# Two-layer mixer and chunk attention: where x's split parts are kept, when projection weights are listed, and how the output steps are spread

## The chip, the cores and the metric

The kernel runs on one core of one Trainium2 chip. The metric is the time of one execution in device microseconds (us). A profiled execution gives, beside its time, a span: from its first to its last instruction on the core.

## The reference

`x` is 2048 rows of 1024 float32. Cut to what matters here:

```python
# layer A
h = rms_norm(x, a_norm_g);  u, v, z = split(h @ w_in, 3)       # 3 x 2048 columns
v = layer_norm(gelu(v));    mixed = per-head 128x128 mixing of v, + b_s
x = x + (gelu(u) * mixed * silu(z)) @ w_out
# shared keys and values, from the same x
k, v = split(rms_norm(x, g_kv) @ w_kv, 2)                        # 16 heads of 64
# layer B: each chunk of 64 rows attends to itself and the 8 chunks before it
h = rms_norm(x, b_norm_g);  q, z = split(h @ w_qz, 2)
p = softmax(q * scale @ k.T + relative bias);  o = p @ v
x = x + (o * silu(z)) @ w_out
return rms_norm(x, final_norm_g)
```

## The kernel before

**Products.** Every float32 product is made of three matmuls of rounded parts (`mm3`, L112): an operand is split into a high part (ScalarE copies it into float32r) and a low part (VectorE subtracts the high part), and high x high, high x low and low x high are summed in one PSUM bank. The large products (layer A, values, layer B's output) use Strassen's scheme: seven sub-products, called phases, `PHS = (1, 7, 2, 6, 5, 4, 3)`, each with two 128-row parts `jp` here.

**Stages.** Layer A comes first and the change leaves it alone. Then the rows go through in four tiles `t` of 512 rows, each of four blocks `b` of 128 rows.

*Value stage.* For each tile, `norm` loads a block of x and normalizes it, `block` transposes it on TensorE and copies the transposed block back in place (`xf[t, b]`, 128 x 8 x 128), and `strassen("vp")` multiplies it with the value weights: 14 products of 4 steps, one step being one `mm3`. Before each product `v_left` splits its left operand with `split_s` into two tiles of the tag `S`, of which the pool `vp` has 8. The operand is a 128 x 512 half of a block as it is (phases 1, 2, 4), or a sum that GpSimd has made in place by then (7, 6, 5, 3). `block` also stores the unsplit transposed block in DRAM (`xtd`), for the attention stage.

*Attention stage.* For each tile, `reload(t)` brings all 512 rows back as the right operands of the projections, in two tiles with one buffer each, `hh` (high parts) and `hl` (low parts): it loads a block into one of four `raw` buffers, copies on ScalarE (L168) and subtracts on VectorE (L169). For each of 8 head pairs `p`, `project` makes q and k, `gate` makes z; each such projection (`one`, 8 steps of 3 matmuls) needs one weight tile, which `weights` loads, scales by the gain where `t` is 0, and splits into two tiles of the tag `T`, 8 in all. `score` makes one 128-row block of scores and its softmax, `flip` transposes and splits it, `value` multiplies with the values.

*Output.* The product with layer B's output weights for tile t-1 (`outs[t-1]`, 56 steps) is run between the heads of tile t. Each phase takes four `T` tiles, loaded by `o_right`; its left operands are sums on four `raw` buffers (`o_left`).

**Order.** One Python loop lists the instructions: for each head pair eight rounds `u`, each with a score, a share of the steps of the generator `ahead(t, p)`, a flip, and again a share. `ahead` lists the projections of the next head pair, then `SHARE[t][p]` steps of the output; at the last head pair of a tile it lists `reload(t + 1)` first, then the output steps, then the first projections of tile t+1. A scheduler places the listed instructions on the engines' queues, so an engine's order can differ from the list; each queue then runs in order. `paced_by_pj` adds an order edge without a wait, so that a weight copy does not come ahead of a given projection matmul. All DMAs are issued from the SP queue.

Of the kernel before, what the change touches and what calls it, by code (L numbers as in the profile page):

```python
# [9 lines left out]
F32 = mybir.dt.float32  # L10
# [7 lines left out]
P = 128  # L18
S = 2048
D = 1024  # L20
KD = D // P
T = 512
NT = S // T
TB = T // P
W2 = 2048
NH = W2 // P
NPAIR = 8
# [6 lines left out]
def trunk_kernel(  # L34
# [19 lines left out]
    nc = tc.nc  # L54

    dram = ctx.enter_context(tc.tile_pool(name="dram", bufs=1, space=DRAM))
# [16 lines left out]
        for t in range(NT - 1)  # L73
    ]
    vhd = [dram.tile([P, NPAIR, TB, 256], F32, name=f"vhd{t}") for t in range(NT)]
    xtd = [[dram.tile([P, D], F32, name=f"xtd{t}_{b}") for b in range(TB)] for t in range(NT)]
    ogd = [dram.tile([P, 2, NPAIR, 2, P], F32, name=f"ogd{t}") for t in range(NT)]
    x2d = [[dram.tile([P, D], F32, name=f"x2d{t}_{b}") for b in range(TB)] for t in range(NT - 1)]

# [7 lines left out]
    kg = cst.tile([P, KD, 1], F32, name="kg")  # L87
    bg = cst.tile([P, KD, 1], F32, name="bg")
# [7 lines left out]
    sh = ctx.enter_context(tc.tile_pool(name="sh", bufs=1))  # L96
# [26 lines left out]
    sub, add = ALU.subtract, ALU.add  # L123
    tv, tg = nc.vector.tensor_tensor, nc.gpsimd.tensor_tensor
# [16 lines left out]
    def x_tiles(t):  # L141
        th = sh.tile([P, KD, T], F32R, tag="hh", name=f"hh_b{t}")
        tl = sh.tile([P, KD, T], F32R, tag="hl", name=f"hl_b{t}")
        xT[t] = [(th[:, k, :], tl[:, k, :]) for k in range(KD)]
        return th, tl

    def block(t, b):
        xt = xf[t, b]
        half = [
            banks[0].tile([P, 4, P], F32, tag="t4", name=f"tr_b{t}_{b}_{h}", bufs=4)  # L150
            for h in range(2)
        ]
        for k in range(KD):
            tpose(half[k // 4][:, k % 4, :], xt[:, k * P : (k + 1) * P], ident[:])
        x3 = xt[:].rearrange("p (k c) -> p k c", k=KD)
        for h in range(2):
            ks = slice(h * 4, h * 4 + 4)
            nc.scalar.copy(x3[:, ks, :], half[h][:])
        nc.sync.dma_start(xtd[t][b][:], xt[:])

    def reload(t):
        th, tl = x_tiles(t)
        for b in range(TB):
            xt = sh.tile([P, D], F32, tag="raw", name=f"xr_b{t}_{b}", bufs=4)
            nc.sync.dma_start(xt[:], xtd[t][b][:])
            x3 = xt[:].rearrange("p (k c) -> p k c", k=KD)
            oh = th[:, :, b * P : (b + 1) * P]
            nc.scalar.copy(oh, x3)  # L168
            tv(tl[:, :, b * P : (b + 1) * P], x3, oh.bitcast(F32), op=sub)  # L169

    pace = []
    beat = []
# [7 lines left out]
            )  # L180
        return ins

    def paced_by_pj(ins, back=2):
        if pace:
            tc.add_manual_dep(
                ins.ins, pace[-min(back, len(pace))],
                mybir.DependencyInfo(mybir.DependencyClass.NoSync, mybir.DependencyReason.DATA),
                reason="order",
            )

    def scaled(raw, gain):
# [11 lines left out]
    def raw_w(t, name):  # L203
        if t:
            return raws[0].tile([P, 1024], F32, tag="wr", name=name, bufs=2)
        return sh.tile([P, 1024], F32, tag="raw", name=name, bufs=4)

    def split_in(raw, wh, wl):
        hi = nc.scalar.copy(wh[:], raw[:])  # L209
        tv(wl[:], raw[:], wh[:].bitcast(F32), op=sub)  # L210
        return hi

    def weights(t, p, c):
        name = f"b{t}_{p}_{c}"
        raw = raw_w(t, f"raw_{name}")
        w = w_tile(f"wh_{name}"), w_tile(f"wl_{name}")
        if t:
            nc.sync.dma_start(raw[:], wk3[p][c][:])
        else:
            nc.sync.dma_start(raw[:], w_kqz[p, :, c, :])  # L220
            paced_by_pj(scaled(raw, (bg if c else kg)[:, :, :]), 3)
            nc.sync.dma_start(wk3[p][c][:], raw[:])
        hi = split_in(raw, *w)
        if t:
            paced_by_pj(hi)
        return w
# [61 lines left out]
            evict(ph, jp, ps[:])  # L288
            yield

    def split_s(pool, bufs, name, src):
        hi, lo = (
            pool.tile([P, 4, P], F32R, tag="S", name=f"S{i}{name}", bufs=bufs) for i in "hl"
        )
        nc.scalar.copy(hi[:], src)
        tv(lo[:], src, hi[:].bitcast(F32), op=sub)
        return [(hi[:, k, :], lo[:, k, :]) for k in range(4)]

    def o_sums(u, place, s_place):
# [43 lines left out]
    with ExitStack() as actx:  # L343
# [21 lines left out]
        sub, add, mul = ALU.subtract, ALU.add, ALU.mult  # L365
# [544 lines left out]
        for n in range(2, 6):  # L910
            b = start[n, 1]
# [46 lines left out]
        tv, tg = nc.vector.tensor_tensor, nc.gpsimd.tensor_tensor  # L958
# [159 lines left out]
    with ExitStack() as vctx:  # L1118
        vp = vctx.enter_context(tc.tile_pool(name="vp", bufs=1, reuse_waits="tile"))
# [16 lines left out]
        def v_left(t):  # L1136
            def raw(jp, r, h):
                return xf[t, 2 * jp + r][:, h * 512 : h * 512 + 512]

            def left(ph, jp):  # L1140
                a11, a12, a21, a22 = (raw(jp, r, h) for r in range(2) for h in range(2))
                src = {1: a11, 7: a11, 2: a12, 6: a11, 5: a21, 4: a22, 3: a12}[ph]
                out = split_s(vp, 8, f"v{t}_{ph}_{jp}", src.rearrange("p (k c) -> p k c", k=4))
                if ph == 1:
                    tg(a11, a11, a21, op=sub)
# [72 lines left out]
    with ExitStack() as bctx:  # L1218
# [16 lines left out]
        def half_tile(tag, name, bufs, dtype=F32):  # L1235
            return sb.tile([P, 512], dtype, tag=tag, name=name, bufs=bufs)

        def c_tile(name):
            return half_tile("C", name, 4)

        def one(t, p, c):
# [350 lines left out]
        def o_all(t):  # L1592
# [158 lines left out]
```

## Time and profile before

| | us |
|---|---|
| median of 3 runs | 2696.48 (2694.29 to 2697.41) |
| profiled execution | 2698.01 |
| its span | 2696.2 |
| TensorE busy in it | 2627.2 (97%) |
| value stage, tiles 0 to 3 | 1351 to 1531 |
| attention stage, tile 0 | 1531 to about 1729 |
| attention stage, tile 1 | to about 2031 |
| attention stage, tile 2 | to about 2318 |
| attention stage, tile 3, and the last output | to 2696 |

Matmuls are pipelined: one of 128 x 512 has a duration of 0.39 us in the rows while the next starts 0.23 us after it, so a matmul that is "busy" is not one that runs alone. Lost time shows as a gap in brackets at the end of a timeline row (the idle time before the instruction, and what ended it), and as matmuls that start 0.43 us apart, when the granted clock is halved (PEclk).

### The profile page before, as it was taken

To read this page: it belongs to the slowest core of one execution; us is meant where nothing else is said; L and a number is where in the kernel's file an instruction comes from. 1 tells how busy PE (TensorE), PEld (TensorE's weight loads), DVE (VectorE), ACT (ScalarE), POOL (GpSimd) and SP (SyncE) were. 2 spreads that over 40 slices of the span, in tenths; PEclk is the share of its full clock that TensorE was granted. 3 is DMA by queue.
4 is the path that set the end of the run, shared out by engine and by line. 5 is a ranking of instruction groups with operands and counts; after the bars stand their busy time and mean duration, and the time that the engine had idled before them with its cause. 6 is when DMAs were issued, how large, how long until landed. Compare 5 with 4: busy or idle time off the path is not lost.

```text
span 2696.2 us, 38071 instructions
## 1 busy us (share of the span) xinstructions
PE 2627.2 (97%) x12960; PEld 2197.9 (82%) x12960; DVE 1892.0 (70%) x2937; ACT 1296.6 (48%) x2296; POOL 888.2 (33%) x874
## 2 busy tenths in 40 slices
PE   9999999999999999999989999999999999999997
PEld 7888888888888888888878788787887888788885
DVE  5655676766777568657677767788677667766676
ACT  5422242443434435333365466676556555655553
POOL 3511335152262414015043344343332223323243
PEclk9999999999999999999999999999999999999999
DMA  7898999989888879858666687788889667766576
GB/s 293 314 326 332 342 364 326 328 306 350 331 320 281 308 259 334 301 200 273 256 238 209 216 266 232 223 294 290 281 265 295 200 220 246 242 204 193 180 236 238
DMA packets 274770, 735.53 MB, mean 273 GB/s; under 512 B 29584, under 2 KB 61328, under 8 KB 274576
## 3 DMA queue, kind: packets, MB, share of 16 engines
q1 hardware_dynamic: 274576, 733.09, 79.2%
q8 instruction: 104, 1.70, 0.2%
q14 instruction: 90, 0.74, 0.1%
HBM read 540.56 MB, written 181.93 MB: 268 GB/s over the span
## 4 chain that ended last, share of the span: by engine, by line
PE 81%; DVE 7%; DMA 6%; issue 2%; ACT 2%; POOL 2%; SPq 1%; DVEq 0%; POOLq 0%; ACTq 0%
PE P L115 11%; PE P L114 11%; PE P L113 11%; PE pj L115 5%; PE pj L113 5%; PE pj L114 5%; PE pv L1391 4%; PE Po L113 4%; PE Po L114 4%; PE Po L115 4%; PE s L1331 4%; PE tp L1366 3%; PE vp L115 1%; PE vp L113 1%; PE vp L114 1%
## 5 line engine op out<-in xcount | busy, mean ns | idle before, releaser
L113 PE MATMUL P<-T,S 128*128 128x512 f32 x1248 | 497.0, 398 | 2.1 <-ACT S L393 2.1
L115 PE MATMUL P<-T,S 128*128 128x512 f32 x1248 | 491.1, 394 | 0.0
L114 PE MATMUL P<-T,S 128*128 128x512 f32 x1248 | 490.1, 393 | 0.6 <-DVE T L396 0.6
L1350 POOL TENSOR_SCALAR pr<-pr,sl 128x640 f32<-128x640 f32 (+4 forms) x256 | 199.3, 779 | 522.9 <-DVE sl L1349 473.8
L113 PE MATMUL pj<-hh_b,wh_b 128*128 128x512 f32 x768 | 320.6, 417 | 1.6 <-ACT hh_b L168 0.8
L115 PE MATMUL pj<-hh_b,wl_b 128*128 128x512 f32 x768 | 305.9, 398 | 0.8 <-DVE wl_b L210 0.7
L114 PE MATMUL pj<-hl_b,wh_b 128*128 128x512 f32 x768 | 304.4, 396 | 0.0
L1346 ACT ACTIVATE pr<-pr,nm 128x640 f32<-128x640 f32 (+4 forms) x256 | 195.4, 763 | 193.2 <-DVE nm L1339 182.4
L115 PEld LDWEIGHTS P<-T,S 128*128 128x128 f32 x1248 | 235.8, 189 | 50.4
L113 PEld LDWEIGHTS P<-T,S 128*128 128x128 f32 x1248 | 236.2, 189 | 46.9 <-ACT S L393 2.3
L114 PEld LDWEIGHTS P<-T,S 128*128 128x128 f32 x1248 | 236.0, 189 | 46.1 <-DVE T L396 1.0
L1371 DVE TENSOR_TENSOR pt<-tp,pt 128x640 fp32r<-128x640 f32 (+4 forms) x256 | 188.7, 737 | 49.2 <-ACT pt L1370 46.2
L1339 DVE CUSTOM_DVE_ANT_0 pr<-s,bias 128x640 f32<-128x640 f32 (+4 forms) x256 | 188.0, 735 | 43.6 <-PE s L1331 36.7
L1370 ACT CAST pt<-tp 128x640 fp32r<-128x640 f32 (+4 forms) x256 | 159.1, 622 | 50.9 <-PE tp L1366 47.3
L1366 PE MATMUL tp<-ident,pr 128*128 128x128 f32 x1120 | 167.8, 276 | 10.4 <-DVE pt L1371 7.9
L115 PEld LDWEIGHTS pj<-hh_b,wl_b 128*128 128x128 f32 x768 | 145.5, 189 | 34.1 <-DVE wl_b L210 2.8
L1366 PEld LDWEIGHTS tp<-ident,pr 128*128 128x128 f32 x1120 | 131.4, 141 | 44.6 <-issue 17.0
L113 PEld LDWEIGHTS pj<-hh_b,wh_b 128*128 128x128 f32 x768 | 146.5, 191 | 20.1 <-ACT wh_b L209 1.6
L1391 PEld LDWEIGHTS pv<-pt,V 128*128 128x128 f32 x896 | 144.2, 190 | 20.2 <-ACT pt L1370 2.6
L114 PEld LDWEIGHTS pj<-hl_b,wh_b 128*128 128x128 f32 x768 | 146.6, 191 | 17.1
L1391 PE MATMUL pv<-pt,V 128*128 128x256 f32 (+3 forms) x896 | 154.4, 321 | 2.7 <-ACT pt L1370 1.8
L210 DVE TENSOR_TENSOR wl_b<-raw_b,wh_b 128x1024 fp32r<-128x1024 f32 x96 | 125.8, 1311 | 26.9 <-ACT wh_b L209 25.3
(283 smaller groups left out, 5739.4 us busy)
## 6 DMA issues: line engine op xcount, KB each, us to landing
S<-hsd SPq DMA_DIRECT2D x288, 512.0 KB, 5.4
rw<-in_w_a SPq DMA_DIRECT2D x108, 512.0 KB, 6.3
A<-ytd SPq DMA_DIRECT2D x72, 512.0 KB, 5.8
raw_b<-wk SPq DMA_DIRECT2D x72, 512.0 KB, 4.4
hsd<-S SPq DMA_DIRECT2D x56, 512.0 KB, 4.3
V<-vhd SPq DMA_DIRECT2D x56, 512.0 KB, 5.7
wh_bo<-ows SPq DMA_DIRECT2D x50, 512.0 KB, 4.7
wl_bo<-ows SPq DMA_DIRECT2D x50, 512.0 KB, 5.8
```

What stands on the lines that cost most here:

```text
L113: first = mm(ps, lh, rh, start=first, stop=False)
L114: mm(ps, lh, rl, start=False, stop=False)
L115: mm(ps, ll, rh, start=False, stop=last)
L210: tv(wl[:], raw[:], wh[:].bitcast(F32), op=sub)
L1331: mm(ps[:, sg, :w], q[:, qb * P : (qb + 1) * P], kx[:, koff + sg * w : koff + (sg + 1) * w], start=i == 0, stop=i == 1,)
L1339: nc.vector.tensor_tensor_reduce(out=pr[:, c0:].rearrange("p (a b) -> p a b", a=nseg), in0=ps[:, :nseg, :w], in1=bias[:, c0:].rearrange("p ...
L1346: nc.scalar.activation(pr[:, c0:], pr[:, c0:], AF.Exp, scale=-1.0, bias=nm[:], accum_out=sl[:])
L1350: nc.gpsimd.tensor_scalar(pr[:, c0:], pr[:, c0:], sl[:], 1.0, op0=ALU.mult, op1=ALU.mult)
L1366: ins = tpose(tp[:, b, :], pr[:, b * P : (b + 1) * P], ident[:])
L1370: nc.scalar.copy(oh, tp[:, b0:5, :].rearrange("p a b -> p (a b)"))
L1371: nc.vector.tensor_tensor(pt[:, 2560 + o + b0 * P : 2560 + o + 640], tp[:, b0:5, :].rearrange("p a b -> p (a b)"), oh.bitcast(F32), op=ALU ...
L1391: mm(po[:, q0 * P : q1 * P], vtl[t, p][:, i, hs], rhs, start=(i == blocks[0] and j == 0), stop=(i == 7 and j == 1),)
```

## The change

- The value stage keeps its split halves. `split_s` can store both parts in DRAM (`keep`), in a new layout `xsd[t]` (128 x 2 x 8 x 512) that is that of `hh` and `hl`. Phases 1, 2 and 4 split three of the four unsplit halves of each pair of blocks anyway; the fourth, `a21`, is split in addition at phase 1, only to be stored. So a tile adds two splits and 16 stores of 256 KB, in pieces of 512 bytes; the four stores of `xtd` (512 KB each, in pieces of 4 KB) go.
- `reload` loads `hh` and `hl` straight from `xsd`: 8 DMAs of 512 KB a tile. Its four `raw` loads, four copies on ScalarE and four subtractions on VectorE go.
- `one` lists the weights of the next projection after the second step of the present one (`row_of` is the order of projections, `w_of` the weights listed). The order edges are named from one projection matmul later, so they point at the same matmuls.
- `SHARE` spreads the 56 output steps anew.

```diff
-    xtd = [[dram.tile([P, D], F32, name=f"xtd{t}_{b}") for b in range(TB)] for t in range(NT)]
+    xsd = [dram.tile([P, 2, KD, T], F32, name=f"xsd{t}") for t in range(NT)]
...
-        nc.sync.dma_start(xtd[t][b][:], xt[:])
...
     def reload(t):
         th, tl = x_tiles(t)
-        for b in range(TB):
-            xt = sh.tile([P, D], F32, tag="raw", name=f"xr_b{t}_{b}", bufs=4)
-            nc.sync.dma_start(xt[:], xtd[t][b][:])
-            x3 = xt[:].rearrange("p (k c) -> p k c", k=KD)
-            oh = th[:, :, b * P : (b + 1) * P]
-            nc.scalar.copy(oh, x3)
-            tv(tl[:, :, b * P : (b + 1) * P], x3, oh.bitcast(F32), op=sub)
+        for k in range(0, KD, 2):
+            for i, x_ in enumerate((th, tl)):
+                nc.sync.dma_start(x_[:, k : k + 2, :].bitcast(F32), xsd[t][:, i, k : k + 2, :])
...
-    def paced_by_pj(ins, back=2):
+    def paced_by_pj(ins, back=1):
...
-            paced_by_pj(scaled(raw, (bg if c else kg)[:, :, :]), 3)
+            paced_by_pj(scaled(raw, (bg if c else kg)[:, :, :]), 2)
...
-    def split_s(pool, bufs, name, src):
+    def split_s(pool, bufs, name, src, keep=None):
...
+        if keep:
+            for i, x_ in enumerate((hi, lo)):
+                nc.sync.dma_start(keep(i), x_[:].bitcast(F32))
...
+                def whole(n, x_, b, k):
+                    cs = slice(b * P, (b + 1) * P)
+                    return split_s(
+                        vp, 8, n, x_.rearrange("p (k c) -> p k c", k=4),
+                        lambda i: xsd[t][:, i, k : k + 4, cs],
+                    )
+
+                if ph in (1, 2, 4):
+                    b, k = {1: (2 * jp, 0), 2: (2 * jp, 4), 4: (2 * jp + 1, 4)}[ph]
+                    out = whole(f"v{t}_{ph}_{jp}", src, b, k)
+                else:
+                    out = split_s(vp, 8, f"v{t}_{ph}_{jp}", src.rearrange("p (k c) -> p k c", k=4))
+                if ph == 1:
+                    whole(f"x{t}_{jp}", a21, 2 * jp + 1, 0)
...
         def one(t, p, c):
-            wh, wl = weights(t, p, c)
+            n = row_of.index((t, p, c))
+            if n not in w_of:
+                w_of[n] = weights(t, p, c)
+            wh, wl = w_of[n]
...
+                if k == 1 and n + 1 < len(row_of):
+                    w_of[n + 1] = weights(*row_of[n + 1])
...
         SHARE = [
-            (0,) * 8, (0, 0, 0, 0, 17, 17, 18, 4), (2, 8, 8, 9, 9, 8, 8, 4), (2, 7, 7, 7, 7, 7, 7, 12)
+            (0,) * 8, (0, 0, 0, 0, 16, 16, 16, 8), (2, 8, 8, 8, 8, 7, 7, 8), (2, 7, 8, 8, 8, 8, 8, 7)
         ]
```

More of the change, by code (lines that the diff above doesn't have):

```diff
@@ L1142, in left @@
                 src = {1: a11, 7: a11, 2: a12, 6: a11, 5: a21, 4: a22, 3: a12}[ph]
-                out = split_s(vp, 8, f"v{t}_{ph}_{jp}", src.rearrange("p (k c) -> p k c", k=4))
+                def whole(n, x_, b, k):
[11 more added lines that the diff above has]
+                    whole(f"x{t}_{jp}", a21, 2 * jp + 1, 0)
                 if ph == 1:
@@ L1239, in c_tile @@
             return half_tile("C", name, 4)
+        row_of = []
+        for t_ in range(NT):
+            for p_ in range(NPAIR):
+                row_of += [(t_, p_, 1), (t_, p_, 0)]
+                if p_:
+                    row_of += [(t_, 0, 2)] * (p_ == 1) + [(t_, p_, 2)]
+        w_of = {}
         def one(t, p, c):
-            wh, wl = weights(t, p, c)
+            n = row_of.index((t, p, c))
+            if n not in w_of:
+                w_of[n] = weights(t, p, c)
+            wh, wl = w_of[n]
             acc = pmm.tile([P, T], F32, tag="mm", name=f"pj{t}_{p}_{c}")
```

## Prediction, made before the changed kernel was run

> **What bounds the kernel now.** I read the page first, then the table of busy time in windows of my choice, then TensorE's timeline where a window showed a loss, and last the other engines' timelines at those places.
>
> ```profile
> span 2696.2 us, 38071 instructions
> PE 2627.2 (97%) x12960; PEld 2197.9 (82%) x12960; DVE 1892.0 (70%) x2937; ACT 1296.6 (48%) x2296; POOL 888.2 (33%) x874
> ```
> TensorE is the bound, so work taken from ScalarE and VectorE is worth nothing by itself; only TensorE's lost time can be won. Windows show where that lies (us, then busy time of PE, PEld, DVE, ACT, POOL, then granted clock, DMA share, GB/s):
>
> ```profile
> 2100.00:2150.00 50.00, 50.00 (x275) 43.30 (x274) 34.37 (x65) 30.25 (x54) 15.14 (x21) 1.00 0.69 212
> 1351.00:1396.00 45.00, 36.56 (x154) 29.40 (x155) 35.38 (x45) 29.43 (x52) 19.27 (x14) 0.89 0.73 262
> 1396.00:1441.00 45.00, 45.00 (x220) 37.69 (x219) 34.51 (x61) 27.47 (x59) 17.39 (x15) 1.00 0.65 220
> 1505.00:1514.00 9.00, 6.78 (x23) 5.14 (x22) 7.83 (x12) 3.32 (x9) 2.14 (x2) 0.81 0.87 294
> 1723.00:1737.00 14.00, 10.80 (x39) 8.44 (x39) 12.78 (x21) 9.37 (x17) 6.18 (x7) 0.76 0.64 214
> 2009.00:2036.00 27.00, 22.24 (x102) 17.93 (x101) 21.97 (x42) 14.96 (x29) 11.86 (x15) 0.87 0.88 303
> 2316.00:2328.00 12.00, 9.73 (x51) 7.73 (x50) 11.26 (x20) 6.72 (x14) 7.22 (x7) 1.00 0.91 288
> 2343.00:2353.00 10.00, 7.58 (x33) 6.18 (x32) 6.44 (x11) 3.69 (x8) 1.09 (x3) 0.83 0.65 232
> 2606.00:2620.00 14.00, 10.48 (x44) 8.77 (x43) 7.58 (x16) 4.81 (x10) 10.39 (x10) 0.76 0.84 304
> ```
> Inside a tile TensorE has no idle time (2100 to 2150, 1396 to 1441). It loses time at the value stage's start, the tile borders and the tail. A window's loss is its idle time plus (1 - clock) times its length, since the clock is halved for a while after a stop: 1505 to 1514 loses 2.2 + 1.7 = 3.9 us; 1723 to 1737, the border of tiles 0 and 1, 3.2 + 3.4 = 6.6; 2009 to 2036, the next border, 4.8 + 3.5 = 8.3; 2316 to 2328, the third, 2.3; 2343 to 2353 2.4 + 1.7 = 4.1; 2606 to 2620 3.5 + 3.4 = 6.9; 1351 to 1396 8.4 + 5.0 = 13.4. These 45 us are what the change can touch.
>
> **Part 1: the reload leaves ScalarE and VectorE.** The rows of TensorE that waited (start, duration, then in brackets the idle time and what ended it), and what the others did:
>
> ```profile
> 1506.15 0.40 PE L113 MATMUL vp<-vwh,Shv 128*128 128x512 f32 x1
> 1508.76 0.79 PE L115 MATMUL vp<-vwh,Slv 128*128 128x512 f32 x1 [2.22 <-DVE Slv L296]
> 1510.20 0.63 PE L115 MATMUL vp<-vwh,Slv 128*128 128x512 f32 x1
> 1510.63 0.63 PE L113 MATMUL vp<-vwh,Shv 128*128 128x512 f32 x1
> 2012.41 0.47 PE L113 MATMUL bo<-wh_bo,Sho 128*128 128x512 f32 x1 [0.97 <-DMA wh_bo<-ows]
> 2013.52 0.50 PE L114 MATMUL bo<-wl_bo,Sho 128*128 128x512 f32 x1 [0.64 <-DMA wl_bo<-ows]
> 2026.27 0.74 PE L1366 MATMUL tp<-ident,pr 128*128 128x128 f32 x5 [0.80 <-DVE pt L1371]
> 2027.52 0.56 PE L1331 MATMUL s<-K,Qh 128*128 128x320 f32 x2 [0.51 <-DVE nm L1339]
> 2030.14 0.74 PE L1366 MATMUL tp<-ident,pr 128*128 128x128 f32 x5 [1.77 <-DVE pt L1371]
> 2320.62 0.74 PE L1366 MATMUL tp<-ident,pr 128*128 128x128 f32 x5 [1.18 <-DVE pt L1371]
> 1500.51 3.50 DVE L169 TENSOR_TENSOR hl_b<-xr_b,hh_b 128x1024 fp32r<-128x1024 f32 x3 [3.46 <-PE vp L115]
> 2018.92 0.42 SPq L165 DMA_DIRECT2D xr_b<-xtd  x1
> 2025.01 0.41 SPq L165 DMA_DIRECT2D xr_b<-xtd  x1
> 2029.87 1.03 ACT L168 CAST hh_b<-xr_b 128x1024 fp32r<-128x1024 f32 x1
> ```
> *Value stage, last tile.* VectorE stood 3.46 us until TensorE released `hl`, then did 3.50 us of reload; the split `Slv` queued behind it came late and TensorE stood 2.22 us, then ran at half clock (matmuls 0.43 us apart). DMAs on SP do this in future, and nothing of the value products is queued behind them but stores and loads needed later. What is late next is the ordinary split, early elsewhere (1396 to 1441 has no gap). **-3.9 us**, bounds -3.9 and 0.
>
> *Border of tiles 1 and 2.* Two of four `raw` loads went out only at 2018.92 and 2025.01, because output operands held the `raw` buffers; the last copy ran at 2029.87, between the softmax instructions for which TensorE then stood (0.80, 0.51, 1.77 us), and half the halved clock, 1.7 us, belongs to that: 4.8 us. Straight loads need no `raw` buffer and can start when `hh` is released, before eight output steps that need no `hh`. The other 3.4 us (0.97 + 0.64 and half the clock) are output weights loaded too late; the new `SHARE` gives the border exactly the last phase, whose weights the head before lists. I take two thirds. **-7.0 us**, bounds -8.3 and 0.
>
> *Border of tiles 2 and 3.* The 1.18 us at 2320.62 follow the same copies; 2343 to 2353 waits for a load of the finished output and stays. **-1.2 us**, bounds -2.3 and +3.
>
> *Border of tiles 0 and 1.* No output step covers it. The loads are priced from these rows (KB each, median us to landing):
>
> ```profile
> 1723.53 0.40 PE L115 MATMUL pj<-hh_b,wl_b 128*128 128x512 f32 x1
> 1728.98 0.80 PE L113 MATMUL pj<-hh_b,wh_b 128*128 128x512 f32 x1 [0.80 <-ACT hh_b L168]
> raw_b<-wk SPq DMA_DIRECT2D x72, 512.0 KB, 4.4
> ogd<-og SPq DMA_DIRECT2D x60, 128.0 KB, 3.4
> wh_bo<-ows SPq DMA_DIRECT2D x50, 512.0 KB, 4.7
> wl_bo<-ows SPq DMA_DIRECT2D x50, 512.0 KB, 5.8
> ```
> `hh` is released at 1723.9 and the first projection began at 1728.98, 5.1 us later. A 512 KB load lands in 4.4 us; the second of a pair comes at the rate of 303 GB/s (window 2009 to 2036) 1.7 us later: 4.4 to 6.1 us for the first quarter, each further quarter 3.5 us. TensorE needs 1.4 us for the six matmuls of a quarter (0.23 us apart in full clock) and about as much for scores and flips between. So the start is equal and the rest up to 1.5 us late three times. All that SP lists behind the 4.2 MB waits up to 14 us: bias, values and stored outputs, whose users are a head away. **+1 us**, bounds -2 and +6.
>
> At this point the Trainium skill differs from the rows. Its page "TensorE: Matmul & The Clock Gate", Part 1, lets the clock fall to half only after about one idle window of 3.4 us. Here a stop of 2.22 us was followed by matmuls 0.43 us apart, so the trace disagrees. By the page's rule the two terms above would be 2.2 and about 4.0 instead of 3.9 and 7.0, and the forecast below 4.7 us later, 2692; since the rows speak against it, it gets no chance of its own.
>
> **Part 2: the value stage keeps its splits.**
>
> ```profile
> L168 ACT CAST hh_b<-xr_b 128x1024 fp32r<-128x1024 f32 x16 | 16.3, 1046 | 0.8 <-DMA xr_b<-xtd 0.8
> L169 DVE TENSOR_TENSOR hl_b<-xr_b,hh_b 128x1024 fp32r<-128x1024 f32 x16 | 20.2, 1289 | 3.5 <-PE vp L115 3.5
> L295 ACT CAST Shv<-bx_b 128x512 fp32r<-128x512 f32 x28 | 17.2, 622 | 11.3 <-PE vp L114 6.8 <-POOL bx_b L1145 4.4
> L296 DVE TENSOR_TENSOR Slv<-bx_b,Shv 128x512 fp32r<-128x512 f32 x28 | 25.3, 918 | 5.6 <-ACT Shv L295 5.6
> 1388.77 0.80 PE L115 MATMUL vp<-vwh,Slv 128*128 128x512 f32 x1 [5.47 <-DVE Slv L296]
> ```
> Eight splits come in: 8 x 0.62 = 5.0 us on ScalarE and 8 x 0.92 = 7.3 us on VectorE, against 16.3 and 20.2 us of reload that go. In tiles 1 to 3 VectorE has 10 us to spare per 45 (1396 to 1441), and the first product of a tile lasts 2.7 us (12 x 0.23), so they are covered; without that cover each costs 0.92. In tile 0 VectorE is the bound behind the 5.47 us stop: its two extra splits, 1.8 us, go straight on the path. Also new: a tile of tag `S` is free only when its stores have landed, and the first two products with their extra splits take all 8. Phase 7's first split waits for phase 1's stores, about 3.4 us or more after its split, just when TensorE arrives. ScalarE stands meanwhile, with that split's successors and the evictions queued behind. The stores' bytes double to 16 MB; the DMA share is 0.73 in tile 0. **+3 us**, bounds 0 and +8.
>
> **Part 3: weights ahead, output steps.** The order edge still names the same matmuls, so the copies cannot start earlier than before; only their place among the others changes.
>
> ```profile
> PE pj L115 <- DVE wl_b L210: 0.7, 3, 0.4
> PE pj L113 <- ACT wh_b L209: 0.7, 1, 0.7
> PE bo L113 <- DMA wh_bo<-ows: 6.1, 3, 3.5
> 2612.41 0.77 PE L113 MATMUL bo<-wh_bo,Sho 128*128 128x512 f32 x1 [3.52 <-DMA wh_bo<-ows]
> ```
> (TensorE's waits: us, times, longest.) All waits for projection weights are 1.4 us, so there is next to nothing to win. The price is `T` tiles: two projections hold 4 and an output phase 4, all 8, so the next phase's weights start later. **+2 us**, bounds -1.4 and +20 (second rival). In the tail the 3.52 us stop waits for output weights; the new last share holds one phase, already loaded, so of 6.9 us I take -4.5, bounds -6.9 and 0. Five steps of three matmuls at 0.23 us, 3.5 us, leave the tail as filler for full stretches: **+1**, bounds 0 and +3.5.
>
> **Sum.** -3.9 - 7.0 - 1.2 + 1 + 3 + 2 - 4.5 + 1 = -9.6 us on the profiled execution's 2698.0 (1.8 us of it outside the span): 2688.4. The median of the runs is 1.5 us lower, so I forecast **2687 us**. Its own terms, the large ones half off, leave 2679 to 2692.
>
> **Rivals.** *The gain is taken back at the start.* The value stage's stores and the uncovered border cost their upper bounds, 8 and 6 us instead of 3 and 1: 2697. For it: the DMA share of 0.73 before the bytes are added. Against it: the next window has 0.65 and no gap. The Trainium skill, page "DMA: Bandwidth & Descriptors", Bandwidth, speaks for it, as it advises at least 1 MiB a DMA, and these stores have a quarter of that; no run here shows yet what they cost in this place. Chance 0.17.
>
> *Output weights become the wait (slower).* With `T` full, the second half of a phase's weights can start only when the phase's first half is free, four steps before it is needed: 12 x 0.23 = 2.8 us, and a flip of 0.7 and a score between, about 3.8 us, against 4.7 to 5.8 us to landing. That is 0.9 to 2.0 us at each of 20 changes of phase. At 1.0 us each the term of +2 becomes +20: 2705. It decides as soon as the landing takes longer than the four steps. For it: these waits are already TensorE's largest of a DMA (6.1 us). Against it: they came three times in 20, with the same tiles, and `T` is only full while projections run. Chance 0.20.
>
> *Listing ahead does nothing*, as its edges are the old ones: then the +2 falls away, 2685. It is inside the forecast.
>
> **How the numbers follow.** Chances: forecast 0.57, gain taken back 0.17, output weights 0.20, other mishaps 0.06. A measurement of this kernel tells 0.2%, 5.4 us, from no change. Faster by more than that holds the forecast, 0.57; within it lies most of the first rival, 0.16; the rest is slower, 0.27. The range runs from 2671, where every removed loss goes whole and part 2 costs nothing, to 2706, just past the second rival.
>
> **What would show it.** Right: no L168 or L169; no stop near the end of the value stage; no wait for `pt` and no halved clock at the border of tiles 1 and 2; the first projection of tile 1 again about 5 us after the last of tile 0. Wrong: waits for `wh_bo` or `wl_bo` at most changes of phase; `Shv` waiting for the landing of `xsd`; a border at which TensorE waits for loads of `hh` by more than 8 us.

## The result: 0.7% slower, and the profile after

The changed kernel takes **2714.93 us** (median of 4 runs, 2709.65 to 2717.76) against 2695.39 us before (4 runs, 2693.93 to 2697.41). The ratio is 1.0070, with a 95% interval of 1.0052 to 1.0087: slower by 19.5 us where 2687 us, a gain of 8 us, was forecast, and outside the range. One of the eleven executions of e3, one of the experiments below, took 12145.2 us and is in no ratio. The page of the profiled execution after (2715.47 us): its span, busy times, and the DMA lines of before and after.

```profile
span 2713.7 us, 38164 instructions
PE 2627.4 (97%) x12960; PEld 2194.2 (81%) x12960; DVE 1864.0 (69%) x2929; ACT 1287.3 (47%) x2288; POOL 882.7 (33%) x874
DMA packets 308562, 752.31 MB, mean 277 GB/s; under 512 B 30608, under 2 KB 95120, under 8 KB 308368
```
```profile
DMA packets 274770, 735.53 MB, mean 273 GB/s; under 512 B 29584, under 2 KB 61328, under 8 KB 274576
```

TensorE is as busy as before (2627.2 us then): its idle time grew from 69.0 to 86.3 us, and that is the growth of the span. The other engines gave up 28, 9 and 6 us, worth nothing, as said. The packets of 512 B to 2 KB doubled: the new stores.

Where it went, by stage. A cell is the time between two first matmuls in TensorE's timeline (value stage: first value product to first projection; "border" runs from the first projection of a tile's last head pair to that of the next tile's third, so it holds the change of tiles and what follows; "tile" is what lies between, and the tail begins with the last projection matmul). "Again" is a second profile of the kernel before, taken with the experiments; the two differ by up to 3 us in a stage. The columns e1 to g2 are experiments, told of below; e8 is the one with GpSimd's queue.

| us | before | again | after | e1 | e2 | e3 | e4 | e7 | e8 | h1 | g2 |
|---|---|---|---|---|---|---|---|---|---|---|---|
| value stage | 179.9 | 177.8 | 182.5 | 180.1 | 177.9 | 180.3 | 181.6 | 179.7 | 181.4 | 177.9 | 180.2 |
| tile 0 | 168.5 | 167.2 | 173.2 | 174.0 | 167.3 | 168.9 | 170.1 | 167.0 | 167.6 | 167.5 | 170.8 |
| border 0/1 | 87.2 | 86.4 | 91.1 | 98.1 | 86.7 | 87.2 | 96.5 | 84.5 | 91.0 | 86.6 | 92.2 |
| tile 1 | 184.7 | 184.8 | 188.8 | 183.8 | 186.8 | 182.3 | 183.5 | 185.1 | 186.3 | 181.3 | 183.6 |
| border 1/2 | 120.6 | 119.6 | 125.6 | 134.6 | 124.0 | 119.9 | 129.4 | 122.5 | 124.1 | 119.8 | 122.3 |
| tile 2 | 183.0 | 183.0 | 182.2 | 183.0 | 184.8 | 181.5 | 181.5 | 181.6 | 181.4 | 183.2 | 181.3 |
| border 2/3 | 110.4 | 107.5 | 107.9 | 109.0 | 109.0 | 110.6 | 112.4 | 108.3 | 115.9 | 105.3 | 115.8 |
| tile 3 | 208.5 | 208.5 | 215.3 | 208.5 | 208.4 | 212.6 | 211.5 | 211.2 | 212.8 | 208.5 | 212.8 |
| tail | 102.0 | 102.0 | 98.1 | 103.4 | 102.8 | 96.1 | 98.0 | 95.9 | 95.1 | 100.5 | 94.6 |

Against the first profile the change cost 2.6 in the value stage, 4.7 in tile 0, 3.9 and 5.0 at the first two borders, 4.1 in tile 1 and 6.8 in tile 3, and gained 0.8, 2.5 and 3.9 in tile 2, at the last border and in the tail: 19.9 us (the span grew by 17.5, layer A being 2.5 us shorter in this profile). Loss came in at six of the nine stages.

Four places after, as TensorE's timeline shows them (start, duration; in brackets the idle time before and what ended it):

```profile
1451.84 0.50 PE L115 MATMUL vp<-vw,Slv 128*128 128x512 f32 x1 [1.63 <-DVE Slv L291]
1456.50 0.51 PE L115 MATMUL vp<-vw,Slv 128*128 128x512 f32 x1 [1.62 <-DVE Slv L291]
1736.05 0.77 PE L113 MATMUL pj<-hh_b,wh_b 128*128 128x512 f32 x1 [2.45 <-DMA hh_b<-xsd]
1980.44 0.50 PE L114 MATMUL bo<-wl_bo,Sho 128*128 128x512 f32 x1 [1.94 <-DMA wl_bo<-ows]
2038.22 0.67 PE L114 MATMUL bo<-wl_bo,Sho 128*128 128x512 f32 x1 [1.96 <-DMA wl_bo<-ows]
2077.55 0.56 PE L1356 MATMUL s<-K,Qh 128*128 128x320 f32 x2 [2.87 <-DVE nm L1364]
```
And two windows (us, busy PE, PEld, DVE, ACT, POOL, granted clock, DMA share, GB/s), the third tile of the value stage and the border of tiles 1 and 2:

```profile
1446.90:1492.50 45.60, 42.35 (x201) 34.68 (x200) 32.09 (x53) 22.64 (x49) 19.27 (x14) 1.00 0.79 245
1984.70:2110.30 125.60, 116.97 (x609) 98.50 (x608) 86.28 (x162) 66.55 (x122) 37.20 (x51) 0.96 0.85 286
```
In the middle tiles of the value stage, which had no gap, TensorE now stands 2 to 3 us each, nearly all of it waiting for splits; the first projection of tile 1 waits for its load; output weights come late in tile 1 (waits for `wl_bo` 7.3 us in 6, against 1.2 in 3); and at the border of tiles 1 and 2, 8.6 us idle and 5.0 at half clock, TensorE waits 4.5 us for output weights, 3.0 for softmax and 1.1 for projection weights.

The DMA issues after (KB each, median us from issue to landing):

```profile
raw_b<-wk SPq DMA_DIRECT2D x72, 512.0 KB, 4.4
hh_b<-xsd SPq DMA_DIRECT2D x16, 512.0 KB, 7.6
hl_b<-xsd SPq DMA_DIRECT2D x16, 512.0 KB, 8.3
xsd<-Shv SPq DMA_DIRECT2D x24, 256.0 KB, 4.0
```
The prediction took 4.4 us for a load of 512 KB. That is the price of one alone. Of eight issued together each comes behind those before it, which makes the medians 7.6 and 8.3: at the border of tiles 0 and 1 they were issued from 1729.19 us on and landed from 1734.6 to 1743.5, 14.3 us after the first issue. The prediction's 6.1 us for the first quarter and 3.5 for each further one make 16.6, so the eight came no slower than priced.

### The profile page after: what moved, and what is told of

Read it like the earlier page. It is cut to its first block, busy times and chain, and to the rows that moved or that the text cites. A ratio compares the mean times of both kernels' runs of the same rounds, so it can differ in the third digit from the quotient of the medians.

```text
span 2713.7 us, 38164 instructions
## 1 busy us (share of the span) xinstructions
PE 2627.4 (97%) x12960; PEld 2194.2 (81%) x12960; DVE 1864.0 (69%) x2929; ACT 1287.3 (47%) x2288; POOL 882.7 (33%) x874
## 5 line engine op out<-in xcount | busy, mean ns | idle before, releaser
L115 PEld LDWEIGHTS P<-T,S 128*128 128x128 f32 x1248 | 234.9, 188 | 50.2
```

Of the source, the lines that this page charges most:

```text
L115: mm(ps, ll, rh, start=False, stop=last)
```

## The experiments

Theories at the start: **A**, listing the weights ahead costs the time (`T` tiles held, output weights late); **B**, the stores and bare loads do; **C**, the shares do. All ratios are to the kernel before on the same chip, with 95% intervals.

### The three parts one by one

e1: parts 1 and 2 alone (`xsd`, `reload`, `split_s` as in the diff above, nothing else). e2: listing ahead alone (`row_of`, `w_of`, back edges). e3: `SHARE` alone. e4: e1 and e3, that is the changed kernel without

```diff
-                if k == 1 and n + 1 < len(row_of):
-                    w_of[n + 1] = weights(*row_of[n + 1])
```

e1: 

> The kernel before with parts 1 and 2 alone: the value stage stores its splits, the reload is loads in place; projection weights and output shares stay as before. Theory A (listing the weights ahead with 8 T tiles costs the time): this kernel keeps what was forecast for the first two parts, 2684 to 2692 us. Theory B (the stores and the bare loads cost the time): 2700 to 2715. Theory C (the shares): about the time before, within 5 us.

e2: 

> The kernel before with projection weights listed one projection ahead, and nothing else. Theory A (weights ahead with 8 T tiles): slower by 12 to 22 us, 2708 to 2717, with waits for output weights in the tiles 1 to 3 and stops inside tile 0. Theory B and theory C: within 3 us of before.

e3: 

> The kernel before with the new table of output steps alone. Theory C (steps taken away from the fourth to sixth head of tile 1 and from the tail cost the time): slower by 8 to 20 us. Theories A and B: faster by 2 to 6 us, since the tail's stop for output weights goes (4.5 us at 2606 to 2620 were forecast).

e4: 

> The changed kernel without the listing ahead: stores of the splits, loads in place, new shares. Theory A: 2680 to 2692 us, faster than both kernels. Theory B: 2700 to 2715. Theory C: slower than before by 5 to 15.

Measured: e1 1.0129 (1.0115 to 1.0143), e2 1.0058 (1.0045 to 1.0070), e3 1.0001 (0.9992 to 1.0010), e4 1.0118 (1.0103 to 1.0134). So B and A both hold, C does not, and no single theory explains the change. The parts don't add: the kernel with all three (1.0070) is 13 us faster than e4, so listing ahead, which costs 14 us by itself, pays back about as much as soon as the loads are there. e3 did not gain the 2 to 6 us expected of it: its tail became 6 us shorter and its tile 3 4 us longer, with 12 more output matmuls in it and a wait for `pt` that before has not (2.3 us). e1 and e4 were beyond the range of theory B (2723.45 and 2720.44 us).

What B is shows at e1's border of tiles 1 and 2. SP's queue there (start, duration, what it issued):

```profile
2013.85 0.38 SPq L236 DMA_DIRECT2D wl_bo<-ows  x1
2017.24 0.32 SPq L1539 DMA_DIRECT2D x2d<-oc  x1
...
2028.49 0.32 SPq L1539 DMA_DIRECT2D x2d<-oc  x1
...
2035.10 0.38 SPq L1539 DMA_DIRECT2D x2d<-ou  x1
2035.53 0.42 SPq L164 DMA_DIRECT2D hh_b<-xsd  x1
2041.47 1.00 SPq L1567 DMA_DIRECT2D out<-y  x2
2042.52 0.44 SPq L1539 DMA_DIRECT2D x2d<-ou  x1
2043.01 0.45 SPq L164 DMA_DIRECT2D hl_b<-xsd  x1
...
2076.25 0.81 SPq L213 DMA_DIRECT2D raw_b<-wk  x1
```
The old x was read for the last time by the projection matmuls from 2012.70 on. Its successor's first load went out at 2035.53 and the others from 2043.01: they stand in one queue behind stores that wait for results of the output product (`x2d<-oc`, `x2d<-ou`, `out<-y`). Behind them in turn come the weights of the next projections, at 2076.25; in the second profile of before the same weights were loaded from 2031.47 on. The order of TensorE's instructions is another too. It is that of the two built programs (s score, tp flip, pj projection; head, round, count), and the timelines show the same sequence of kinds and counts from 2049.0 us on before and from 2067.6 in e1:

```
before: tp_15_1 x5, s_0_0 x1, pj_1_1 x4, s_0_0 x3, pj_1_1 x4, tp_15_2 x5, pj_1_1 x4, s_0_1 x4, pj_1_1 x7, tp_15_3 x5, s_0_2 x4, ...
e1:     tp_15_1 x5, s_0_0 x4, s_0_1 x4, tp_15_2 x5, s_0_2 x4, tp_15_3 x5, s_0_3 x4, tp_0_0 x5, s_1_0 x4, s_1_1 x4, pj_1_1 x2, ...
```
Two windows show what that costs: the stretch in e1 with all instructions, then its projections alone (us, then busy PE, PEld, DVE, ACT, granted clock, DMA share, GB/s; POOL before the clock in the first).

```profile
2067.60:2084.50 16.90, 10.96 (x45) 8.32 (x44) 10.69 (x27) 9.52 (x19) 5.46 (x9) 0.66 0.94 320
```
```profile
2067.60:2084.50 16.90, 0.02 (x1) 0.00 (x0) 1.38 (x2) 1.16 (x2) 0.66 0.94 320
```
In 16.9 us there is no projection but the tail of one. Scores and flips follow each other and TensorE waits for softmax between them (`nm`, `sl`, `pt`): 5.9 us idle and (1 - 0.66) x 16.9 = 5.7 us of half clock, in which idle time at half clock is counted twice. By the same count the whole border loses 25 us in e1 and 10 before, so this stretch is nearly half of e1's loss there. In before the same ten groups of scores and flips stand between projections.

The x loads themselves were not what the projection behind that stretch waited for: all eight had landed by 2056.8 us. It began at 2084.53, once its weights, issued at 2076.25 and landed at 2081.5, had been split. In the changed kernel the listing ahead sends the same weights out at 2004.02, before the loads, and that projection begins at 2060.77. That is how the listing pays there.

The timelines of all runs bear the order out. A stretch of 44 matmuls of scores and flips without any other product stands in e1, e4 and the later s12 and v, 16.9 to 18.4 us long; the changed kernel has one of 18 (6.4 us); before, e3 and e7 have none over 15. But it is not the whole: both kernels of e8 have none either and are slower than before, and e2, which has no such loads, has one of 29 (7.9 us).

### Is it the place in the queue (D) or the transfers (E)?

e6: the reload listed one head earlier, without listing ahead; the same in the changed kernel. e7: half of the loads left out. e8: another queue for the loads, GpSimd's and then ScalarE's. f2: two loads of 2 MB.

```diff
@@ e6, in ahead; its old place at the last head goes @@
                 yield from gate(t, p + 1)
+                if p + 2 == NPAIR and t + 1 < NT:
+                    reload(t + 1)
@@ e7, in reload; the loads of tl go @@
+        xT[t] = [(th[:, k, :], th[:, k, :]) for k in range(KD)]
@@ e8, in reload @@
-                nc.sync.dma_start(x_[:, k : k + 2, :].bitcast(F32), xsd[t][:, i, k : k + 2, :])
+                nc.gpsimd.dma_start(x_[:, k : k + 2, :].bitcast(F32), xsd[t][:, i, k : k + 2, :])
@@ f2, in reload, for the eight loads @@
+        for i, x_ in enumerate((th, tl)):
+            nc.sync.dma_start(x_[:].bitcast(F32), xsd[t][:, i])
```

e6: 

> Stores of the splits, loads in place and new shares, without listing ahead (ratio 1.0118 as measured), with the reload listed one head earlier: behind the last projection that reads the old x, ahead of the output steps of the seventh head, so that its loads stand on the SP queue ahead of the stores of finished output. Theory D (the loads stand on the one SP queue behind stores that wait for results, the first projections come late and rounds of softmax run alone): the 17 us behind the border of tiles 1 and 2 go, the 8 us behind the border of tiles 0 and 1 stay; 2695 to 2703. Theory E (the bytes of the loads cost the time): no change, 2715 to 2722.

e6, all parts: 

> The changed kernel, all three parts, with the reload listed one head earlier in the same way. Theory D: the 10 to 13 us behind the border of tiles 1 and 2 go; the waits for wl_bo in tile 1 stay (7 us); 2696 to 2704. Theory E: as the changed kernel, ratio 1.007.

e7: 

> As the kernel with stores, loads in place and new shares without listing ahead (ratio 1.0118), but with the loads of the low parts left out: hl is hh, four loads of 512 KB a tile instead of eight. Its values are therefore not the reference's. Theory D (place in the queue): the loads still stand behind the output stores, so the border of tiles 1 and 2 keeps at least half of its 17 us; 2708 to 2718. Theory E (bytes): the loads take 7 us instead of 14, both borders fall by half or more; 2698 to 2708.

e8, GpSimd: 

> Stores of the splits, loads in place and new shares without listing ahead (ratio 1.0118), with the eight loads of each reload issued by GpSimd instead of SP: same bytes, same pieces, another queue. Theory D (the one SP queue: the loads delay the weight loads behind them, so that projections are ordered behind rounds of softmax): no run of softmax rounds without a projection at the tile borders, ratio 0.997 to 1.002. Theory E (bytes and contention of the loads): 1.008 to 1.013.

e8, ScalarE: 

> The same with the loads issued by ScalarE. Theory D: 0.998 to 1.003, a little behind the GpSimd one, since a load that waits for the old x holds up the copies and exponentials queued behind it. Theory E: 1.008 to 1.013.

f2: 

> Stores of the splits, loads in place and new shares without listing ahead (ratio 1.0118), with each reload made of two loads of 2 MB instead of eight of 512 KB: same bytes. Theory D (place on the queue and the order that follows): in this kernel's order the projections behind the border of tiles 0 and 1 are no longer put behind rounds of softmax, while behind the border of tiles 1 and 2 they still are; so the first border (87 us from the eighth head of tile 0 to the third of tile 1 before, 96.5 with eight loads) falls below 90 and the second stays near 129. Theory E (the transfers): the first stays at 95 or more. By the advice of the Trainium skill, page DMA: Bandwidth & Descriptors, section Bandwidth, of 1 MiB or more for a DMA, both borders would gain.

Measured: e6 1.0095 (1.0079 to 1.0112) and, with all parts, 1.0097 (1.0080 to 1.0114); e7 **1.0002** (0.9989 to 1.0015); e8 1.0076 (1.0055 to 1.0097) on GpSimd's queue and 1.0125 (1.0104 to 1.0146) on ScalarE's; f2 1.0103 (1.0085 to 1.0122).

Without half of the loads the whole loss is gone, more than either theory said. On GpSimd's queue the bytes are the same, the built order at all three borders mixes projections and softmax as before, and 0.0042 of the ratio (11 us, the intervals apart) is gone: that much is place and order, a clear miss of D, which expected all of it. ScalarE's queue gains nothing: the value stage took 190.2 us there, where a split of ScalarE stood behind the loads of the first reload and TensorE waited 6.99 us for it. The other 20 us remain with the same bytes. So neither theory is enough by itself. That the transfers cost those 20 us is argued and not shown: e7's order is the mixed one too, so it cannot part the two, and in e8 GpSimd issues the loads beside its own work and is busy 15 us longer in the three borders than in e4 (116.2 against 101.4). e8 keeps waits that before hasn't. Its TensorE at the first two borders:

```profile
1728.63 0.77 PE L113 MATMUL pj<-hh_b,wh_b 128*128 128x512 f32 x1 [2.06 <-DMA hh_b<-xsd]
1748.12 0.38 PE L1343 MATMUL s<-K,Qh 128*128 128x320 f32 x1 [2.11 <-DMA Qh<-Qh]
2024.53 0.49 PE L114 MATMUL bo<-wl_bo,Sho 128*128 128x512 f32 x1 [4.71 <-DMA wl_bo<-ows]
```
Three transfers came late, two of them not of x at all. e8's third border is 5.5 and 8.4 us longer than in the two profiles of before; why stays open.

f2 parts the first border in two. With eight loads (e4) the way from the border's start to the first projection of tile 1 is 30.9 us and from there to the border's end 65.6, against 29.0 and 57.5 in the second profile of before. With two loads it is 38.7 and 58.4: e4's run of 21 scores and flips (9.4 us) is gone from order and time (7 us), and the first projection waits for a whole 2 MB, 10.39 us where e4 waits 1.99:

```profile
1746.59 0.77 PE L113 MATMUL pj<-hh_b,wh_b 128*128 128x512 f32 x1 [10.39 <-DMA hh_b<-xsd]
```
Theory D expected the border under 90 us; it is 97, as theory E had it, though the order changed as D said. The Trainium skill, page "DMA: Bandwidth & Descriptors", Bandwidth, advises 1 MiB or more for a DMA; no gain from it shows here (1.0103 against 1.0118, intervals overlapping): with eight loads TensorE starts on the first quarter.

e6 put its eight loads where the prediction had them, right behind the last reader, and the order behind the border of tiles 1 and 2 became the mixed one:

```profile
2006.97 0.32 SPq L164 DMA_DIRECT2D hl_b<-xsd  x1
2007.39 0.86 SPq L164 DMA_DIRECT2D hh_b<-xsd  x2
...
2010.55 0.43 SPq L164 DMA_DIRECT2D hl_b<-xsd  x1
```
That border fell from 129.4 to 125.9 us, not to 120, and e6's 2718.2 us lie in the range of theory E, with an interval that touches e4's. The next weights went out at 2054.31, behind the stores of finished output, and TensorE waited for them (1.71 us for `wh_b` at 2060.69). In the kernel with all parts the early listing gained nothing (1.0097 against 1.0070, intervals overlapping), where D expected 2696 to 2704 us: tile 1 took 190.1 us against 188.8, and the third border rose from 107.9 to 116.6.

### What listing ahead costs

e5: two more weight tiles. h1: nothing listed ahead across output steps. g2: h1's line in the changed kernel.

```diff
@@ e5, in weights @@
+        if turn % 2:
+            w = [raws[0].tile([P, 1024], F32R, tag="TW", name=f"w{i}_{name}", bufs=2) for i in "hl"]
@@ h1 and g2, in one @@
-                if k == 1 and n + 1 < len(row_of):
+                if k == 1 and n + 1 < len(row_of) and not (t and p and c == 2):
```

e5: 

> The kernel before with weights listed ahead (as the kernel that had this alone, ratio 1.0058), and two weight tiles more: every second projection's pair gets its own tag, so that projections and output phases hold up to 10 instead of 8. Room for them comes from two small tiles of the attention stage that are written in place instead. Theory A (the weights ahead cost time because the 8 tiles of tag T run out): the waits for wh_bo fall from 12.0 us to under 5 and the time to within 5 us of before. Rival (the order, not the tiles): it stays 10 to 15 us slower than before.

h1: 

> The kernel before with weights listed ahead (ratio 1.0058 when alone), but not across output steps: the last projection of a head lists nothing ahead from tile 1 on. Theory A (two weight tiles held through the output steps starve the output's weights): waits for wh_bo fall to about 6 us as before, ratio 0.999 to 1.002. Rival (the place of the copies among the softmax work costs the time): 1.004 to 1.006.

g2: 

> The changed kernel with weights listed ahead only within a head, not across output steps. If the tiles held through the output steps cost 10 us in the changed kernel as they did alone (1.0058 against 0.9993): ratio 1.002 to 1.005. If the gain of listing ahead at the borders needs the listing across output steps: 1.007 to 1.011.

Measured: e5 1.0043 (1.0028 to 1.0059), h1 **0.9993** (0.9982 to 1.0005), g2 1.0058 (1.0041 to 1.0075). TensorE's waits for output weights (us, times, longest) in e2, e5 and h1:

```profile
PE bo L113 <- DMA wh_bo<-ows: 12.0, 6, 3.3
```
```profile
PE bo L111 <- DMA wh_bo<-ows: 9.6, 4, 3.6
```
```profile
PE bo L113 <- DMA wh_bo<-ows: 4.6, 2, 3.0
```
h1 shows that all of e2's loss comes from listing the next head's first weights ahead of the output steps, through which two `T` tiles are then held. That it is the number of `T` tiles, as the second rival had it, is not shown: with ten of them the waits fell by only 2.4 us, the time stayed 11.7 us above before, as the rival had it, and the ratio's interval overlaps e2's. e5 isn't clean: its value stage is 4.6 us and its tile 0 6 us longer than e2's, perhaps by the tiles that it writes in place to make room. In the changed kernel the same line is worth 3 us by the medians of ratios, within the intervals, although tile 1 is 5 us shorter; its third border is 8 us longer. g2's ratio lies in neither of the ranges expected.

### The value stage

s12: 12 instead of 8 tiles of tag `S`, on e4. v: the added splits left out, on e4; phase 5 stores its own split in their place.

```diff
@@ s12, in left @@
-                        vp, 8, n, x_.rearrange("p (k c) -> p k c", k=4),
+                        vp, 12, n, x_.rearrange("p (k c) -> p k c", k=4),
@@ v, in left @@
-                if ph == 1:
-                    whole(f"x{t}_{jp}", a21, 2 * jp + 1, 0)
```

s12: 

> Stores of the splits, loads in place and new shares without listing ahead (ratio 1.0118), with 12 instead of 8 tiles of tag S in the value stage. If the middle tiles of the value stage (44.5 and 45.8 us against 41.8 and 41.9 before) wait for S tiles whose stores have not landed: both back to 42 or 43, ratio about 1.010. If it is the time of the added splits on VectorE: 44 to 46 as now, no change.

v: 

> Stores of the splits, loads in place and new shares without listing ahead (ratio 1.0118; middle value tiles 44.5 and 45.8 us against 41.8 and 41.9), with the two added splits of each tile left out: phase 5 stores its own split in the place of a21's, so the bytes and the number of stores stay and the values are not the reference's. If the added splits at a tile's start make the stops there: both tiles 42 to 43, ratio 1.009 to 1.011. If the stores or the order they bring do: 44 to 46 as now.

Measured: s12 1.0120 (1.0103 to 1.0137), its value stage 185.7 us; v 1.0089 (1.0073 to 1.0105), its value stage 177.8 us, as in the second profile of before. Neither settles it. The middle tiles took 51.4 and 42.0 us in s12, 50.2 and 41.7 in v (e4: 44.5 and 45.7): in both the third tile is back where it was and the second has one long stop of TensorE for the norm of a block (7.56 and 5.73 us), which e4 has not. v's stage is 3.8 us shorter than e4's (181.6), but its first tile alone is 5.0 shorter, and its ratio's interval touches e4's. Splits do wait for stores to land, as this row of ScalarE after shows; there are six such waits there, 8.4 us in all, and none before:

```profile
1493.43 0.62 ACT L290 CAST Shx<-xo_b 128x512 fp32r<-128x512 f32 x1 [2.44 <-DMA xsd<-Shx]
```
The two stops of TensorE shown above, at 1451.84 and 1456.50, end with splits that VectorE reached late, as its rows show:

```profile
1451.10 0.68 DVE L291 TENSOR_TENSOR Slv<-bx_b,Shv 128x512 fp32r<-128x512 f32 x1
1451.70 0.68 DVE L291 TENSOR_TENSOR Slx<-bx_b,Shx 128x512 fp32r<-128x512 f32 x1
1452.30 2.94 DVE L1181 TENSOR_TENSOR v<-vu,v 128x256 fp32r<-128x256 f32 x2
1455.17 0.68 DVE L1209 TENSOR_TENSOR vu<-vp,vu 128x512 f32<-128x512 f32 x1
1455.77 0.67 DVE L291 TENSOR_TENSOR Slv<-bx_b,Shv 128x512 fp32r<-128x512 f32 x1
```
Here, at a tile's start, VectorE has no pause: the last tile's outputs (`v`), the next norms and now `Slx` stand ahead of the `Slv` that TensorE needs. The 10 us to spare per tile lie elsewhere. How much of the stage's loss is this and how much the landings stays open.

### Versions that might beat both

`best`: before with h1's listing and the new `SHARE`. `last`: the same with only the last row of the new `SHARE`.

```diff
-            (0,) * 8, (0, 0, 0, 0, 17, 17, 18, 4), (2, 8, 8, 9, 9, 8, 8, 4), (2, 7, 7, 7, 7, 7, 7, 12)
+            (0,) * 8, (0, 0, 0, 0, 17, 17, 18, 4), (2, 8, 8, 9, 9, 8, 8, 4), (2, 7, 8, 8, 8, 8, 8, 7)
```

best: 

> The kernel before with two parts that alone cost nothing: weights listed ahead only within a head (0.9993) and the new shares (1.0001). No stores or loads of x's parts. If their gains add (2 us, and 6 us of the tail of which 5 were given back): 0.997 to 1.000; if the shares' eight steps at the border undo the listing: 1.000 to 1.003.

last: 

> The kernel before with weights listed ahead only within a head, and of the new shares only those of the last tile (2, 7, 8, 8, 8, 8, 8, 7). The tail loses its stop for output weights (6 us in the kernel with all new shares), five steps more in full heads cost 3.5 us, and the border of tiles 2 and 3, 8 us longer with eight steps there, stays as before: ratio 0.997 to 0.9995, ahead of both kernels. Rival: the order shifts by as much elsewhere, 0.9995 to 1.002.

Measured: 1.0006 (0.9995 to 1.0017) and 0.9991 (0.9980 to 1.0001). The last tile's shares take 5.4 us from the tail (96.6) and give back 4.0 in tile 3. Neither, nor h1, is told from before; no run beat it.

For the second profile of before: 

> The kernel before, unchanged, for a profile on the chip of these runs: 2685 to 2696 us, with its value stage, tiles and tail as in the first profile within 3 us each.

 It took 2691.14 us. Its span is 6.8 us under that of the first profile (value stage 2.1 and layer B 5.7 shorter, layer A 0.9 longer), so 2 or 3 us in a stage between two single profiles are no finding by themselves.

## Why the prediction was wrong, step by step

- **Border of tiles 1 and 2, -7.0: the step that failed.** "Straight loads need no `raw` buffer and can start when `hh` is released" was true of the data and false of the queue. After, the first of eight loads went out at 2014.24, the other seven from 2032.16 on, behind `x2d<-oc` and `x2d<-ou`; in e1 all came from 2035.53 on. Of the old reload's four loads two had gone out at 1969.24 and 1974.28, before those stores; the other two, which the prediction put down to `raw` buffers, directly follow a store in the queue of before too (`x2d<-ou` at 2018.49, `out<-y` at 2023.91). Instead of -7.0 the border cost 5.0, in e4 8.8 and in e1 14.0; that is 12 of the 29.5 us between the forecast's -9.6 and the stages' 19.9. No wait for `pt` is left there, as said, but the waits for output weights rose from 1.6 to 4.5 us. The prediction had weighed the waits of TensorE and not the order of the queues; that projections would come so late that softmax runs alone was on no list of rivals.
- **Border of tiles 0 and 1, +1 (bounds -2 and +6).** After 3.9, alone (e1) 10.9. The loads were priced right (14.3 us for eight). The start was priced as equal and came 1.6 us late, behind a wait of 2.45 us for `hh`; the rest lies behind it, in e1 mostly at a run of 21 scores and flips (9.6 us).
- **Border of tiles 2 and 3, -1.2:** -2.5 after, though the second profile of before has no more than after (107.5 and 107.9 us), so this is no finding.
- **Value stage, last tile, -3.9:** L169 and its stop are gone, the last tile is 39.2 us against 42.2. But the second profile of before has the same 2.22 us stop without halved clock and 40.6: 1.7 us of the term were of that one execution.
- **Part 2, +3 (0 to 8):** about +5.6 (2.6 for the stage, with 3.0 gained in its last tile). The size was within bounds. Splits waited for stores, as said; and the added splits, said to be covered in tiles 1 to 3, stand ahead of the ordinary ones for which TensorE stops twice in tile 2. How the loss parts between the two is open.
- **Part 3, +2, and its rival of 2705.** Alone the listing gave 2703.69 us: the second rival's time, but with 6 stops of 2 us, not 20 of 1. h1 names its place, held tiles across output steps; that 8 tiles are too few stays open. In the changed kernel the same listing took 13 us off e4 by the ratios. By stages of the two profiles it gains 14 us at the three borders, at the second by sending weights out ahead of the loads, and costs about as much in the tiles.
- **Tail, -4.5:** -3.9 after, -5.9 alone. Right. (The prediction's sum for a window counts idle time at half clock twice; in the windows behind its terms that is 0.5 us at most.) **Filler, +1 (0 to 3.5):** 4.1 in tile 3 of e3 and 6.8 after. The 12 output matmuls more are 2.8 us of it, within the bounds; the wait for `pt` (2.3 and 4.8 us) was not in the sum. So the shares come to nothing (1.0001).
- **The first rival**, the gain taken back at the start, was right in direction: the border of tiles 0 and 1 passed its bound of 6 us without listing ahead (9.3 in e4, 10.9 in e1); the value stage, at 5.6 after, stayed under its 8, and it had the border of tiles 1 and 2 on the wrong side.
- **The signs:** no L168 and L169, and no stop near the end of the value stage, as said. The first projection of tile 1 came 7.05 us after the last of tile 0 (1729.00 to 1736.05; before 5.45); a halved clock at the border of tiles 1 and 2 stayed. Of the signs of being wrong, waits for output weights came, but nearly all in tile 1; `Shv` waited for landings of `xsd`; no border waited more than 8 us for `hh`.

What stays open: the 2.4 us more that TensorE stands in tile 0, after as in e4 (most of the rest of the 4.7 there is half clock, of which e4 has none); the 8 us of the third border in e8 and g2 against after; the value stage's cause; and whether fewer bytes or the order that they bring make e7 as fast as before.

## What to carry to other kernels

A load that replaces a copy doesn't start when its buffer is free but when its place on the queue comes: read what stands ahead of it there, above all stores that wait for results, and what stands behind it. Where a scheduler writes the order, another set of transfers can move work on other engines too, as here (why it chose so is not known); compare the built orders around each border before the times. Test parts of a change one by one, since here two that cost 34 and 14 us cost 19.5 together.

## What the runs showed of the hardware

The same stop has two prices. In the second profile of before TensorE stood 2.22 us at the place of the prediction's first term, and ran on at full clock (0.23 us apart), where the first profile had half clock:

```profile
1509.14 0.50 PE L115 MATMUL vp<-vwh,Slv 128*128 128x512 f32 x1 [2.22 <-DVE Slv L296]
1509.48 0.39 PE L113 MATMUL vp<-vwh,Shv 128*128 128x512 f32 x1
1509.71 0.40 PE L114 MATMUL vp<-vwl,Shv 128*128 128x512 f32 x1
```
And the softmax run of e1 fell to a granted clock of 0.66 with no stop over 1.3 us in it, 5.9 us of 16.9 in small ones. So the length of a stop does not decide it here.

What decides it shows in the granted clock itself. In all 20 profiles it changes only at points of a grid of 3.41 us. The windows of that grid around the stop (us, busy time of PE, granted clock, DMA share, GB/s), in the first profile and then in the second:

```profile
1501.98:1505.40 3.42, 3.42 (x17) 1.00 0.66 180
1505.40:1508.81 3.41, 1.19 (x6) 1.00 0.78 285
1508.81:1512.22 3.41, 3.41 (x8) 0.50 0.87 317
```
```profile
1505.21:1508.62 3.41, 1.72 (x8) 1.00 0.85 298
1508.62:1512.03 3.41, 2.88 (x13) 1.00 0.81 297
```
In the first profile the stop lies within one window, in which TensorE is 35% busy, and the next is at half clock; in the second the grid cuts the stop in two, 50% and 84% busy, and the clock stays. Counted over all profiles, 15490 windows at full clock: of the 15111 in which TensorE was at least 60% busy none was followed by half clock, of the 158 under 40% every one was, and in between 73 of 221. e1's fall came after a window 52% busy in small pieces (1.79 of 3.41 us). So a stop of about 2 us costs 1.7 us more or not by where the grid happens to lie, and that part of the prediction's -3.9 was luck.

The Trainium skill, page "TensorE: Matmul & The Clock Gate", Part 1, has the clock fall after about one idle window of 3.4 us: the traces agree with the length of the window, and not with its being idle throughout, since windows 35% and 52% busy were enough.
